# Two-layer hybrid decoder: SBUF slots claimed in a fixed order, and the opening's loads and splits rearranged

## The chip, the cores and the metric

One core of a Trainium2 chip (trn2). The metric is device time in microseconds (us) of one execution, as the median of several runs. Of one execution there is also a profile, with the start and length of every instruction and DMA packet.

## What is computed

A decoder of two layers over 256 tokens of width 1024, all in float32. Cut to what matters:

```python
for l in range(2):
    h = rmsnorm(x, norm_mix[l])                      # x is (1, 256, 1024)
    proj = h @ w_in[l]                               # 1024 x 5956, split into 12 parts
    # indexer parts -> rope -> scores -> 64 best keys per query
    # attention over these keys, q and k normed and roped  -> y_attn
    # HGRN2 gated linear recurrence, 4 heads of 128        -> y_hgrn
    merged = sigmoid(ga) * (y_attn @ w_proj_attn[l]) + sigmoid(gb) * (y_hgrn @ w_proj_hgrn[l])
    x = x + merged @ w_out[l]                        # 1024 x 1024
    g, u = split(rmsnorm(x, norm_ffn[l]) @ w_ffn_in[l])   # 1024 x 5632
    x = x + (silu(g) * u) @ w_ffn_out[l]             # 2816 x 1024
```

The rope angles come from `positions` (256 integers) times 32 inverse frequencies, by sine and cosine.

## The kernel before, in words

Tokens are taken as two row tiles (`i` = 0, 1) of 128. Each weight matrix is read once, in chunks (`take`): a chunk lands in a `w` tile, ScalarE rounds it to `hi` (type fp32r), VectorE subtracts to get `lo`, and each 128 x 128 by 128 x 512 product is three TensorE matmuls (`mm3`): hi weights by hi activations, lo weights by hi activations, hi weights by lo activations. The weight chunk is the moving operand; the transposed activations, split in the same way, are the stationary one. They lie in slots of the tag `hT` (normed input, attention output, merged, second norm) or `s4` (`act`, the FFN's inner activations). There are 3,024 such matmuls of 512 columns, and 96 of 324 columns (`idx`, the first group of each layer; in layer 0 it comes in four chunks).

The program is recorded first and then ordered by a planner (`schedule`, `run`): it keeps one queue per engine, gives each operation a `tail` (the longest path of priced work to the end) plus its `rank`, and at each step starts, on the engine that can start first, the ready operation with the largest sum. The order it finds is fixed in the program, and each engine works through its own list in order: an instruction that waits holds all behind it on that engine. Loads go to SyncE (SP) or, if written so, to GpSimd (POOL).

SBUF memory: each operation's tiles have a tag and a slot, and `emit` asks the pool for the slot when its first user comes up in the order. Addresses therefore go up from byte 16,512 in the order of first use, each slot rounded up to 32 bytes. In the compiled kernel before, this puts the `hT` slots at bytes 67,520, 79,808, 105,408, 117,696 (multiples of 64) and 179,168, 183,264, 203,744, 207,840 (multiples of 64 plus 32); of the `act` tiles some slots are of the first kind, some of the second. Of the 3,024 matmuls of 512 columns, 1,008 have a stationary operand of the second kind. In layer 0's FFN these are all with `i` = 1 (`h2T` of row tile 1 at 203,744 and 207,840), half of its `fi` matmuls; in layer 1's FFN none of the `fi` matmuls. The weight slots `hi` and `lo` all start at odd multiples of 64. The 324-column chunks hold rows of 1,296 bytes, so their moving operands start at steps of 16 bytes within 64.

The opening, up to the first `idx` matmul (lines 525 to 711): `ident` (for transposes), `grow` (norm weights) and the input `x` in three loads are issued on SP, then the weight chunks `w0`, `w1`, ...; nine small loads (positions `posi`, frequencies `invf`, masks `mi`, `vis`, `odd`, norm weights `qkn`, `rows`) on POOL. `WARM` = 24 matmuls of zeros (`gate`) are given the lowest rank and fill TensorE's gaps. Each quarter of `x` (row tile `i`, half `g`) is transposed on TensorE and split from PSUM in four pieces of 128 columns: `hT_hi` on ScalarE and `hT_lo` on VectorE, both with the norm weight of the piece (`gcol`) as scale. VectorE casts `posi` to `posf` and works out the angle tables (`ang`, `kk`, `cosang`, `rc`, `rs`, masks `cm`).

Of the kernel before, what the change touches and what calls it, by code (L numbers as in the profile page):

```python
# [26 lines left out]
N_IDX = 324  # L27
C_HQ, C_HF, C_HV, C_HG, C_GA, C_GB = 1860, 2372, 2884, 3396, 3908, 4932
FIRST = {(0, C_IDX): 2, (0, C_AQ): 2}
WARM = 24  # L30
LEVELS = (2, 4, 8)
TWO_PI = 2.0 * np.pi

# [120 lines left out]
class Program:  # L154
# [98 lines left out]


    def latency(self, a, b):
        if a.eng in ("SP", "POOL") and a.calls[0][0] == "dma_start":
            return self.LAT_DMA
        if a.eng == b.eng:
            return 0.0 if a.eng == "PE" else self.LAT_OWN
        return self.LAT  # L260
# [36 lines left out]
    def run(self, bonus):  # L297
# [63 lines left out]
        while len(order) < len(ops):  # L361
            best = None
            for e, lst in avail.items():
                cand = []
                for o in lst:
                    if o.blocked == releases and o.order != first_left:
                        continue
                    st = slot_time(o)
                    if st is not None:
                        cand.append((max(free[e], ready_at[o], st), o))  # L370
                while cand:
                    t0 = min(c[0] for c in cand)
                    if best is not None and t0 >= best[0]:
                        break
                    here = [(o.tail + o.extra + (bonus if e == "ACT" and o.table in (None, table) else 0.0), -o.order, o)
                            for at, o in cand if at <= t0 + 1.0]
                    o = max(here)[2]
                    if o.order != first_left and any(t.slot is None for t in o.tiles) and not safe(o):
                        o.blocked = releases
                        cand = [c for c in cand if c[1] is not o]  # L380
                        continue
                    best = (t0, o)
                    break
            if best is None:
                raise RuntimeError("no instruction can start")
            t0, o = best
            e = o.eng
            avail[e].remove(o)
            cost = o.cost
            if e == "ACT" and o.table not in (None, table):  # L390
                table = o.table
                cost += self.TABLE
            if o.calls[0][0] == "dma_start":
                begin = max(t0 + 1100.0, dma_free)
                end = begin + cost
                dma_free = end
                free[e] = t0 + (475.0 if e == "SP" else 1040.0)
            else:
                end = t0 + cost
                free[e] = end  # L400
            o.start, o.end, o.done = t0, end, True
            while first_left < len(ops) and ops[first_left].done:
                first_left += 1
            order.append(o)
            for t in o.tiles:
                if t.slot is None:
                    fr = slots[t.tag]
                    fr.sort()
                    t.slot = max((x for x in fr if x[0] <= t0 + 1.0), default=fr[0])[1]
                    fr[:] = [x for x in fr if x[1] != t.slot]  # L410
                    o.first.append(t)
                    live.add(t)
                t.left -= 1
                t.end = max(t.end, end + (self.LAT_DMA if o.calls[0][0] == "dma_start" else self.LAT))
                if t.left == 0:
                    slots[t.tag].append((t.end, t.slot))
                    live.discard(t)
                    releases += 1
            for s in o.succs:
                todo[s] -= 1  # L420
                ready_at[s] = max(ready_at[s], end + self.latency(o, s))
                if not todo[s]:
                    avail[s.eng].append(s)
# [2 lines left out]
        return self.span  # L426


    def emit(self, tc):
        nc = tc.nc  # L430
        engines = {"DVE": nc.vector, "ACT": nc.scalar, "PE": nc.tensor, "SP": nc.sync, "POOL": nc.gpsimd}
        with ExitStack() as ctx:
            sb = ctx.enter_context(tc.tile_pool(name="sb", bufs=1))
            ps = ctx.enter_context(tc.tile_pool(name="ps", bufs=1, space=PSUM))
            ctx.enter_context(tc.manual_schedule())
            real = lambda v: v.resolve() if isinstance(v, View) else v
            for o in self.order:
                for t in o.first:
                    pool = ps if t.tag in PSUM_TAGS else sb
                    t.handle = pool.tile([128] + list(t.shape), t.dtype, tag=f"{t.tag}_{t.slot}", name=t.name)  # L440
                for name, a, k in o.calls:
                    getattr(engines[o.eng], name)(*[real(x) for x in a], **{n: real(x) for n, x in k.items()})  # L442


PSUM_TAGS = ("P", "Q")
SLOTS = {"w": 3, "hi": 3, "lo": 3, "hT": 8, "s4": 14, "s2": 6, "sm": 14, "work": 2, "bias": 2, "rqs": 4,
         "gbc": 2, "P": 4, "Q": 4}
TUNING = {"stretch": 1.5, "bonus": 3000.0, "slack": 4000.0}
# [2 lines left out]
def hybrid_trunk(prog, x_d, pos_d, w_in, w_pa, w_ph, w_out, n_mix, n_ffn,  # L451
# [73 lines left out]

    x = const("x", [NT, D], F32)
    ident = const("ident", [128], F32)
    vis = const("vis", [256], F32)
    cm = const("cm", [4, 512], U8)
    odd = const("odd", [64])  # L530
    gbc = {}

    def load_g(key, src):
# [7 lines left out]

    zero = tmp("zero", [256], BF16)
    V.memset(zero, 0.0)
    touch = small("touch")
    S.activation(touch[:, 0:1], zero[:, 0:1], AF.Copy)
    gate = bank("gate")
    for _ in range(WARM):
        PE.matmul(gate[:, 0:256], zero[:, 0:128], zero, start=True, stop=True)
    prog.rank = 2e6
    grow = tmp("grow", [128])  # L550
    SP.dma_start(grow[0:8, :], n_mix[0].rearrange("(k d) -> k d", k=8))
    SP.dma_start(ident, cf_d[:, 0:128])
    prog.rank = 1e6
    for g in range(2):
        gs = slice(g * 512, (g + 1) * 512)
        SP.dma_start(x[:, 0, gs], x_d[0, 0:128, gs])
    SP.dma_start(x[:, 1, :], x_d[0, 128:256, :])
    prog.rank = 0.0
    neg = const("neg", [256], F32)


# [31 lines left out]
    def norm_half(i, g, gkey, hT, ssq, tag):  # L593

        xs = x[:, i, g * 512:(g + 1) * 512]
        pt = bank(f"xT{i}{g}", tag)
        pv = pt.rearrange("p (k t) -> p k t", k=4)
        if gkey is None:
            transpose4(pt, xs)
            for k in range(4):  # L600
                split_to(hT[i][0][:, g * 4 + k, :], hT[i][1][:, g * 4 + k, :], pv[:, k, :], gcol[:, g * 4 + k:g * 4 + k + 1])
        else:
            xg = tmp(f"xg{i}{g}", [512])
            V.tensor_tensor(xg, xs, gbc[gkey][:, g * 512:(g + 1) * 512], op=ALU.mult)
            transpose4(pt, xg)
            split_to(hT[i][0][:, g * 4:g * 4 + 4, :], hT[i][1][:, g * 4:g * 4 + 4, :], pv)
        junk = tmp(f"sq{i}{g}", [512])
        S.activation(junk, xs, AF.Square, accum_out=ssq[:, g:g + 1])

# [8 lines left out]
    gcol = const("gcol", [8])  # L618
    V.tensor_copy(gcol, growp[:, 0:8])
    hT = pair("hT0")  # L620
    R = []
    for i in range(NT):
        ssq = small(f"ss{i}")
        for g in range(2):
            norm_half(i, g, None, hT, ssq, "P")
        R.append(norm_scale(ssq, f"r{i}"))


    mi = tmp("mi", [320], I32)
    posi = const("posi", [NT], I32)  # L630
    POOL.dma_start(posi, pos_d.rearrange("o (i p) -> p (o i)", p=128))
    invf = const("invf", [32], F32)
    POOL.dma_start(invf, invf_d[0].partition_broadcast(128))
    qkn = const("qkn", [2, DEPTH, 64], F32)
    POOL.dma_start(qkn[:, 0], q_norm.partition_broadcast(128))
    POOL.dma_start(qkn[:, 1], k_norm.partition_broadcast(128))
    POOL.dma_start(vis, cf_d[:, 128:384])
    POOL.dma_start(mi, cm_d)
    POOL.dma_start(odd, cf_d[:, 384:448])
    rows = tmp("rows", [128])  # L640
    V.memset(rows, 0.0)
    POOL.dma_start(rows[0:8, :], h_lb.rearrange("l (h d) -> (l h) d", h=4))
    POOL.dma_start(rows[8:10, :], h_norm)

    V.tensor_scalar(neg, vis, -1.0, BIG, op0=ALU.add, op1=ALU.mult)
    for a in range(3):
        V.tensor_copy(cm[:, a, :].rearrange("p (h t) -> p h t", h=8), mi[:, None, a * 64:a * 64 + 64].to_broadcast([128, 8, 64]))
    V.tensor_copy(cm[:, 3, :].rearrange("p (h t) -> p h t", h=4), mi[:, None, 192:320].to_broadcast([128, 4, 128]))
    posf = small("posf")
    V.tensor_copy(posf[:, 0:NT], posi)  # L650
    ang = tmp("ang", [NT, 32])
    for i in range(NT):
        V.tensor_scalar(ang[:, i, :], invf, posf[:, i:i + 1], None, op0=ALU.mult)
# [25 lines left out]
    for l in range(DEPTH):  # L679
        for a in range(2):  # L680
# [4 lines left out]
                V.tensor_tensor(s_t[:, i, 0:32], IS[:, i, 0:32], qkn[:, a, l, 32:64], op=ALU.mult)  # L685
                V.tensor_tensor(s_t[:, i, 32:64], IS[:, i, 32:64], qkn[:, a, l, 0:32], op=ALU.mult)
            rtab[l, a] = (c_t, s_t)

    colp = bank("colp")
    PE.transpose(colp[:, 0:128], rows, ident)  # L690
    cols = const("cols", [16], F32)
    V.tensor_copy(cols[:, 0:10], colp[:, 0:10])
    lbt = const("lbt", [16], F32)
    V.tensor_tensor(lbt[:, 8:12], cols[:, 0:4], cols[:, 4:8], op=ALU.max)
    V.tensor_tensor(lbt[:, 0:4], cols[:, 0:4], lbt[:, 8:12], op=ALU.subtract)
# [480 lines left out]
```

## Time and profile before

| | |
|---|---|
| Median of 3 runs | 821.86 us (820.89 to 822.17) |
| The profiled execution's own time | 822.42 us |
| Its span in the trace | 820.5 us |
| Mean granted TensorE clock | 0.992 |
| HBM traffic | 137.95 MB read, 169 GB/s over the span |

"Busy" is the time in which an engine worked on at least one instruction; matmuls overlap in the records, so the length of one (0.39 us) is more than the distance from its start to the next one's start. What a matmul costs in a stream is that distance. The granted clock is the share of 2.4 GHz that TensorE had: 1.00 or 0.50 (1.2 GHz).

### The profile page before, as it was taken

To read this page: it belongs to the slowest core of one execution; us is meant where nothing else is said; L and a number is where in the kernel's file an instruction comes from. 1 tells how busy PE (TensorE), PEld (TensorE's weight loads), DVE (VectorE), ACT (ScalarE), POOL (GpSimd) and SP (SyncE) were. 2 spreads that over 40 slices of the span, in tenths; PEclk is the share of its full clock that TensorE was granted. 3 is DMA by queue.
4 is the path that set the end of the run, shared out by engine and by line. 5 is a ranking of instruction groups with operands and counts; after the bars stand their busy time and mean duration, and the time that the engine had idled before them with its cause. 6 is when DMAs were issued, how large, how long until landed. Compare 5 with 4: busy or idle time off the path is not lost.

```text
span 820.5 us, 10255 instructions
## 1 busy us (share of the span) xinstructions
PE 807.7 (98%) x3982; PEld 659.8 (80%) x3982; DVE 537.8 (66%) x947; ACT 403.2 (49%) x518; POOL 5.3 (1%) x13
## 2 busy tenths in 40 slices
PE   7999999999999999999999999999999999999998
PEld 5887788888878888888887778888887888888886
DVE  5999855677775454554488998566868645556442
ACT  5765855343364445452346676533435544445330
POOL 2000000000000000000000000000000000000000
PEclk7999999999999999999999999999999999999999
DMA  8645455333656556546546365543354665655531
GB/s 277 207 148 203 146 174 196 103 112 123 218 190 204 175 185 194 167 153 206 166 154 231 103 206 189 170 146 112 103 195 155 214 198 166 201 179 180 175 133 51
DMA packets 86224, 139.66 MB, mean 170 GB/s; under 512 B 3214, under 2 KB 50480, under 8 KB 86176
## 3 DMA queue, kind: packets, MB, share of 16 engines
q1 hardware_dynamic: 85856, 138.53, 50.9%
q0 software_dynamic: 320, 0.48, 0.3%
q8 instruction: 31, 0.51, 0.3%
q14 instruction: 17, 0.14, 0.0%
HBM read 137.95 MB, written 1.05 MB: 169 GB/s over the span
## 4 chain that ended last, share of the span: by engine, by line
PE 89%; DVE 6%; issue 2%; ACT 2%; DMA 1%; POOL 0%; DVEq 0%; POOLq 0%
PE fi L442 29%; PE fo L442 15%; PE pj L442 5%; PE gb L442 5%; PE wo L442 5%; PE ga L442 4%; PE av L442 3%; PE aq L442 3%; PE hg L442 3%; PE vh L442 3%; PE hq L442 2%; DVE lo L442 2%; PE ak L442 2%; PE idx L442 2%; PE hf L442 1%
## 5 line engine op out<-in xcount | busy, mean ns | idle before, releaser
L442 DVE TENSOR_TENSOR lo<-w,hi 128x2048 fp32r<-128x2048 f32 (+3 forms) x134 | 295.0, 2202 | 222.0 <-ACT hi L442 221.6
L442 ACT ACTIVATE hi<-w 128x2048 fp32r<-128x2048 f32 (+3 forms) x134 | 247.4, 1846 | 284.7 <-PE fi L442 96.4
L442 PE MATMUL fi<-hi,h2T_hi 128*128 128x512 f32 x352 | 141.1, 401 | 0.2
L442 PE MATMUL fi<-hi,h2T_lo 128*128 128x512 f32 x352 | 138.2, 393 | 0.0
L442 PE MATMUL fi<-lo,h2T_hi 128*128 128x512 f32 x352 | 137.7, 391 | 0.0
L442 PE MATMUL fo<-hi,act 128*128 128x512 f32 x352 | 111.4, 395 | 0.0
L442 PEld LDWEIGHTS fi<-hi,h2T_lo 128*128 128x128 f32 x352 | 66.1, 188 | 15.3 <-DVE h2T_lo L442 0.7
L442 PEld LDWEIGHTS fo<-hi,act 128*128 128x128 f32 x352 | 66.1, 188 | 14.9
L442 PEld LDWEIGHTS fi<-hi,h2T_hi 128*128 128x128 f32 x352 | 66.1, 188 | 13.8 <-DVE h2T_lo L442 0.8
L442 PEld LDWEIGHTS fi<-lo,h2T_hi 128*128 128x128 f32 x352 | 66.2, 188 | 13.2
L442 PE MATMUL fo<-lo,act 128*128 128x512 f32 x176 | 69.1, 392 | 0.0
L442 PEld LDWEIGHTS fo<-lo,act 128*128 128x128 f32 x176 | 33.1, 188 | 7.4
L442 PE MATMUL gb<-hi,hT_hi 128*128 128x512 f32 x64 | 26.8, 418 | 0.0
L442 PE MATMUL pj<-hi,yT_hi 128*128 128x512 f32 x64 | 26.0, 407 | 0.0
L442 PE MATMUL wo<-hi,mT_hi 128*128 128x512 f32 x64 | 25.8, 404 | 0.0
L442 PE MATMUL ga<-hi,hT_hi 128*128 128x512 f32 x64 | 25.7, 402 | 0.0
L442 PE MATMUL pj<-hi,yT_lo 128*128 128x512 f32 x64 | 25.3, 395 | 0.0
L442 PE MATMUL pj<-lo,yT_hi 128*128 128x512 f32 x64 | 25.2, 394 | 0.0
L442 PE MATMUL gb<-hi,hT_lo 128*128 128x512 f32 x64 | 25.2, 393 | 0.0
L442 PE MATMUL ga<-hi,hT_lo 128*128 128x512 f32 x64 | 25.1, 393 | 0.0
L442 PE MATMUL wo<-lo,mT_hi 128*128 128x512 f32 x64 | 25.1, 392 | 0.0
L442 PE MATMUL ga<-lo,hT_hi 128*128 128x512 f32 x64 | 25.1, 392 | 0.0
(346 smaller groups left out, 1309.9 us busy)
## 6 DMA issues: line engine op xcount, KB each, us to landing
w<-in_w_ffn_in_dram SPq DMA_DIRECT2D x88, 512.0 KB, 4.7
w<-in_w_in_dram SPq DMA_DIRECT2D x42, 1024.0 KB, 5.1
w<-in_w_ffn_out_dram SPq DMA_DIRECT2D x22, 1024.0 KB, 4.7
w<-in_w_out_dram SPq DMA_DIRECT2D x8, 1024.0 KB, 4.7
w<-in_w_proj_attn_dram SPq DMA_DIRECT2D x4, 1024.0 KB, 4.9
w<-in_w_proj_hgrn_dram SPq DMA_DIRECT2D x4, 1024.0 KB, 4.9
w<-in_w_in_dram SPq DMA_DIRECT2D x4, 512.0 KB, 11.4
w<-in_w_in_dram SPq DMA_DIRECT2D x4, 324.0 KB, 10.8
```

Of the source, the lines that this page charges most:

```text
L442: getattr(engines[o.eng], name)(*[real(x) for x in a], **{n: real(x) for n, x in k.items()})
```

## The change

1. A new method `homes` is called before the first instruction: it claims all SBUF slots in a chosen order. Slots are sorted by size; the small ones fill bytes 16,512 to 24,576, then come `w`, `hi`, `lo` (8,192 bytes each), `hT`, `s4`, `gbc` (4,096 bytes each) from 24,576 on, so that each of these starts at a multiple of 4,096; then the rest.
2. `ident` and `grow` are loaded from ScalarE's queue. `x` is loaded in four quarters; the first goes ahead of everything on SP, the other three get ranks just under those of `w0`, `w1`, `w2`.
3. The small loads move from POOL to SP, with a rank between those of `w1` and `w2`. `vis`, `odd` and `invf` become parts of one tile, `table`.
4. The first splits: transposes of one quarter, one VectorE multiply of 128 x 512 by `gcol` into SBUF (`xg`), one ScalarE copy to `hT_hi`, one subtract to `hT_lo` - on VectorE for the first quarter, on GpSimd for the other three. The squares for the norm come after all of them.
5. Positions are loaded as two rows of 128 integers into the tile that also holds `rows`, converted on GpSimd, turned into columns by the transpose that `rows` needs anyway, and copied out on VectorE.
6. `WARM` is 28; the planner counts ScalarE's DMA issues as it does SP's.

```diff
-WARM = 24
+WARM = 28
...
+    def homes(self, pool):
+        size = {}
+        for tag, q in self.queue.items():
+            for t in q:
+                if tag not in PSUM_TAGS:
+                    key = (tag, t.slot)
+                    size[key] = max(size.get(key, 0), t.n * SIZE.get(t.dtype, 4))
+        big = [k for tag in ("w", "hi", "lo", "hT", "s4", "gbc") for k in sorted(size) if k[0] == tag]
+        rest = sorted((k for k in size if k not in big), key=lambda k: (size[k], k))
+        at, low = BASE, []
+        for k in rest:
+            n = -(-size[k] // 32) * 32
+            if at + n <= ORIGIN:
+                low.append((k, size[k]))
+                at += n
+        low.reverse()
+        named = {k for k, _ in low}
+        if at < ORIGIN:
+            low.append((("pad", 0), ORIGIN - at))
+        for (tag, slot), n in low + [(k, size[k]) for k in big + [k for k in reversed(rest) if k not in named]]:
+            pool.tile([128, -(-n // 4)], F32, tag=f"{tag}_{slot}", name=f"home_{tag}{slot}")
...
+            self.homes(sb)
...
+BASE, ORIGIN = 16512, 24576
...
+    prog.rank = 2e6
+    S.dma_start(ident, cf_d[:, 0:128])
+    S.dma_start(grow[0:8, :], n_mix[0].rearrange("(k d) -> k d", k=8))
+    for g in range(2):
+        for i in range(NT):
+            prog.rank = (2e6, 499500.0)[g + i > 0] - 1e3 * (2 * g + i - 1)
+            gs = slice(g * 512, (g + 1) * 512)
+            SP.dma_start(x[:, i, gs], x_d[0, i * 128:(i + 1) * 128, gs])
...
-            for k in range(4):
-                split_to(hT[i][0][:, g * 4 + k, :], hT[i][1][:, g * 4 + k, :], pv[:, k, :], gcol[:, g * 4 + k:g * 4 + k + 1])
...
+    for g in range(2):
+        ks = slice(g * 4, g * 4 + 4)
+        for i in range(NT):
+            pt = bank(f"xT{i}{g}", "P")
+            transpose4(pt, x[:, i, g * 512:(g + 1) * 512])
+            xg = tmp(f"xg{i}{g}", [4, 128])
+            V.tensor_tensor(xg, pt.rearrange("p (k t) -> p k t", k=4), gcol[:, ks, None].to_broadcast([128, 4, 128]), op=ALU.mult)
+            first_hi = S.activation(hT[i][0][:, ks, :], xg, AF.Copy)
+            E = V if g == 0 and i == 0 else POOL
+            E.tensor_tensor(hT[i][1][:, ks, :], xg, hT[i][0][:, ks, :].bitcast(F32), op=ALU.subtract)
...
+        prog.after = first_hi
+            S.activation(junk, x[:, i, g * 512:(g + 1) * 512], AF.Square, accum_out=ssq[:, g:g + 1])
...
-    POOL.dma_start(posi, pos_d.rearrange("o (i p) -> p (o i)", p=128))
-    POOL.dma_start(invf, invf_d[0].partition_broadcast(128))
...
+    prog.rank = 5e5 - 1e3 * 1.5
+    SP.dma_start(rows[0:8, :], h_lb.rearrange("l (h d) -> (l h) d", h=4))
+    SP.dma_start(rows[8:10, :], h_norm)
+    SP.dma_start(posi[32:34, :], pos_d.rearrange("o (i p) -> (o i) p", p=128))
+    SP.dma_start(table[:, 320:352], invf_d[0].partition_broadcast(128))
+    SP.dma_start(table[:, 0:320], cf_d[:, 128:448])
+    SP.dma_start(mi, cm_d)
+    SP.dma_start(qkn[:, 0], q_norm.partition_broadcast(128))
+    SP.dma_start(qkn[:, 1], k_norm.partition_broadcast(128))
...
+    POOL.tensor_copy(rows[32:34, :], posi[32:34, :])
+    PE.transpose(colp[:, 0:128], rows, ident)
+    V.tensor_copy(cols[:, 0:10], colp[:, 0:10])
+    V.tensor_copy(posf[:, 0:NT], colp[:, 32:32 + NT])
```

## Rows read from the trace of the kernel before

**Rows 1.** Page, busy time, share of the span and instructions of each engine.
```profile
PE 807.7 (98%) x3982; PEld 659.8 (80%) x3982; DVE 537.8 (66%) x947; ACT 403.2 (49%) x518; POOL 5.3 (1%) x13
```
**Rows 2.** Page, the chain of work that ended last, by engine.
```profile
PE 89%; DVE 6%; issue 2%; ACT 2%; DMA 1%; POOL 0%; DVEq 0%; POOLq 0%
```
**Rows 3.** Windows: stretch, length, then each engine's busy time, clock, DMA.
```profile
0.00:5.80 5.80, 4.74 (x22) 3.13 (x22) 0.54 (x4) 2.21 (x4) 4.75 (x12) 1.00 0.38 104
5.80:9.20 3.40, 1.44 (x11) 0.88 (x9) 0.84 (x5) 1.50 (x5) 0.56 (x2) 1.00 0.88 271
9.20:19.50 10.30, 7.75 (x28) 6.89 (x29) 8.67 (x28) 7.66 (x21) 0.00 (x0) 0.51 1.05 365
...
60.00:63.80 3.80, 1.66 (x13) 1.24 (x11) 3.80 (x11) 2.94 (x3) 0.00 (x0) 1.00 0.00 0
63.80:67.30 3.50, 3.50 (x12) 2.73 (x10) 3.50 (x20) 2.89 (x5) 0.00 (x0) 0.52 0.67 209
67.30:82.00 14.70, 14.70 (x80) 11.96 (x79) 14.70 (x45) 6.81 (x7) 0.00 (x0) 1.00 0.67 233
```
**Rows 4.** Timeline, opening: start, length, engine, instruction, idle before and what ended it.
```profile
1.59 1.30 SPq L442 DMA_DIRECT2D x<-in_x_dram  x3
...
2.94 13.03 SPq L442 DMA_DIRECT2D w<-in_w_in_dram  x11
...
4.76 1.06 PE L442 MATMUL xT<-ident,x 128*128 128x128 f32 x4
4.91 0.17 DVE L442 CAST posf<-posi 128x2 f32<-128x2 int32 x1 [3.77 <-DMA posi<-in_positions_dram]
...
8.25 0.39 DVE L442 TENSOR_SCALAR ang<-invf,posf 128x32 f32<-128x32 f32 x2 [3.11 <-DMA invf<-in_invf_dram]
...
9.80 1.97 PE L442 MATMUL xT<-ident,x 128*128 128x128 f32 x8 [2.54 <-DMA x<-in_x_dram]
...
12.51 0.74 ACT L442 ACTIVATE hi<-w 128x648 fp32r<-128x648 f32 x1
...
13.41 0.61 PE L442 MATMUL idx<-hi,hT_hi 128*128 128x324 f32 x1 [1.21 <-DVE hT_lo L442]
```
**Rows 5.** Chain in order of time: start, length, link (first two `idx`/`aq` links).
```profile
14.75 9.41 PE idx L442 x47
24.16 5.48 PE aq L442 x24
```
**Rows 6.** DMA, 0 to 40 us: GB/s in 40 slices of 1 us; then time to landing.
```profile
GB/s 0 39 51 288 164 68 85 360 392 381 344 260 322 388 392 389 387 389 385 389 383 387 389 389 395 350 268 133 27 0 0 0 96 262 412 279 0 0 41 209
...
x<-in_x_dram SPq DMA_DIRECT2D x2, 256.0 KB, 3.5
```
**Rows 7.** Lines of VectorE, 0 to 82 us: count, busy and mean ns, idle before.
```profile
L442 DVE SCALAR_TENSOR_TENSOR hT_lo<-xT,gcol,hT_hi 128x128 fp32r<-128x128 f32 x16 | 4.6, 343 | 0.9 <-ACT hT_hi L442 0.9
...
L442 DVE TENSOR_TENSOR rot<-raw,rc 128x512 f32<-128x512 f32 x4 | 2.7, 678 | 0.0
```
**Rows 8.** Timeline of TensorE, `idx`: the first and last of 12, then of 23.
```profile
16.27 0.47 PE L442 MATMUL idx<-hi,hT_hi 128*128 128x324 f32 x1
...
19.24 0.47 PE L442 MATMUL idx<-hi,hT_lo 128*128 128x324 f32 x1
...
20.58 0.31 PE L442 MATMUL idx<-lo,hT_hi 128*128 128x324 f32 x1
...
23.85 0.31 PE L442 MATMUL idx<-hi,hT_lo 128*128 128x324 f32 x1
```
**Rows 9.** Timeline of TensorE, layer 0's FFN: each first of 12 matmuls.
```profile
303.01 0.39 PE L442 MATMUL fi<-hi,h2T_hi 128*128 128x512 f32 x1
...
305.74 0.39 PE L442 MATMUL fi<-hi,h2T_hi 128*128 128x512 f32 x1
...
308.53 0.39 PE L442 MATMUL fi<-hi,h2T_hi 128*128 128x512 f32 x1
```
**Rows 10.** Chain in order of time, the same stage in layer 0 and layer 1.
```profile
301.77 8.29 PE fi L442 x36
...
678.70 8.19 PE fi L442 x36
```

More of the change, by code (lines that the diff above doesn't have):

```diff
@@ L255, in latency @@
     def latency(self, a, b):
-        if a.eng in ("SP", "POOL") and a.calls[0][0] == "dma_start":
+        if a.eng in ("SP", "POOL", "ACT") and a.calls[0][0] == "dma_start":
             return self.LAT_DMA
@@ L396, in run @@
                 dma_free = end
-                free[e] = t0 + (475.0 if e == "SP" else 1040.0)
+                free[e] = t0 + (1040.0 if e == "POOL" else 475.0)
             else:
@@ L445 @@
 PSUM_TAGS = ("P", "Q")
+SIZE = {U8: 1, BF16: 2}
+BASE, ORIGIN = 16512, 24576
 SLOTS = {"w": 3, "hi": 3, "lo": 3, "hT": 8, "s4": 14, "s2": 6, "sm": 14, "work": 2, "bias": 2, "rqs": 4,
@@ L527, in hybrid_trunk @@
     ident = const("ident", [128], F32)
-    vis = const("vis", [256], F32)
+    table = const("table", [352], F32)
+    vis, odd, invf = table[:, 0:256], table[:, 256:320], table[:, 320:352]
     cm = const("cm", [4, 512], U8)
-    odd = const("odd", [64])
     gbc = {}
@@ L543, in hybrid_trunk @@
     V.memset(zero, 0.0)
+    prog.rank = 2e6
+    grow = tmp("grow", [128])
+    S.dma_start(ident, cf_d[:, 0:128])
[5 more added lines that the diff above has]
+            SP.dma_start(x[:, i, gs], x_d[0, i * 128:(i + 1) * 128, gs])
+    prog.rank = 0.0
     touch = small("touch")
@@ L548, in hybrid_trunk @@
         PE.matmul(gate[:, 0:256], zero[:, 0:128], zero, start=True, stop=True)
[L549 to L558, printed above, removed]
     neg = const("neg", [256], F32)
@@ L597, in norm_half @@
         pv = pt.rearrange("p (k t) -> p k t", k=4)
-        if gkey is None:
-            transpose4(pt, xs)
-            for k in range(4):
-                split_to(hT[i][0][:, g * 4 + k, :], hT[i][1][:, g * 4 + k, :], pv[:, k, :], gcol[:, g * 4 + k:g * 4 + k + 1])
[L602 to L606, printed above, removed]
+        xg = tmp(f"xg{i}{g}", [512])
+        V.tensor_tensor(xg, xs, gbc[gkey][:, g * 512:(g + 1) * 512], op=ALU.mult)
+        transpose4(pt, xg)
+        split_to(hT[i][0][:, g * 4:g * 4 + 4, :], hT[i][1][:, g * 4:g * 4 + 4, :], pv)
         junk = tmp(f"sq{i}{g}", [512])
@@ L623, in hybrid_trunk @@
         ssq = small(f"ss{i}")
+        prog.after = first_hi
         for g in range(2):
-            norm_half(i, g, None, hT, ssq, "P")
+            junk = tmp(f"sq{i}{g}", [512])
+            S.activation(junk, x[:, i, g * 512:(g + 1) * 512], AF.Square, accum_out=ssq[:, g:g + 1])
+        prog.after = None
         R.append(norm_scale(ssq, f"r{i}"))
     mi = tmp("mi", [320], I32)
-    posi = const("posi", [NT], I32)
-    POOL.dma_start(posi, pos_d.rearrange("o (i p) -> p (o i)", p=128))
-    invf = const("invf", [32], F32)
-    POOL.dma_start(invf, invf_d[0].partition_broadcast(128))
     qkn = const("qkn", [2, DEPTH, 64], F32)
[L635 to L639, printed above, removed]
     rows = tmp("rows", [128])
+    posi = tmp("posi", [128], I32)
     V.memset(rows, 0.0)
-    POOL.dma_start(rows[0:8, :], h_lb.rearrange("l (h d) -> (l h) d", h=4))
-    POOL.dma_start(rows[8:10, :], h_norm)
+    prog.rank = 5e5 - 1e3 * 1.5
[7 more added lines that the diff above has]
+    SP.dma_start(qkn[:, 1], k_norm.partition_broadcast(128))
+    prog.rank = 0.0
+    POOL.tensor_copy(rows[32:34, :], posi[32:34, :])
+    colp = bank("colp")
+    PE.transpose(colp[:, 0:128], rows, ident)
+    cols = const("cols", [16], F32)
+    V.tensor_copy(cols[:, 0:10], colp[:, 0:10])
+    posf = small("posf")
+    V.tensor_copy(posf[:, 0:NT], colp[:, 32:32 + NT])
     V.tensor_scalar(neg, vis, -1.0, BIG, op0=ALU.add, op1=ALU.mult)
@@ L648, in hybrid_trunk @@
     V.tensor_copy(cm[:, 3, :].rearrange("p (h t) -> p h t", h=4), mi[:, None, 192:320].to_broadcast([128, 4, 128]))
-    posf = small("posf")
-    V.tensor_copy(posf[:, 0:NT], posi)
     ang = tmp("ang", [NT, 32])
@@ L687, in hybrid_trunk @@
             rtab[l, a] = (c_t, s_t)
[L689 to L692, printed above, removed]
     lbt = const("lbt", [16], F32)
```

## The prediction, made before the changed kernel was run

> **What bounds the kernel now.** I read the busy shares first: TensorE (PE) works in 98% of the span, VectorE (DVE) in 66% [rows 1]. The chain of waits agrees: 89% of the time that led to the end is PE's, 6% is DVE's [rows 2]. So the time is the distance from one matmul to the next, summed, and an edit counts if it shortens that distance or takes away a stretch in which PE stands or runs at half clock. The windows show two such stretches [rows 3]. Up to 19.5 us PE is busy for 13.9 us only, and from 9.2 to 19.5 us the granted clock is 0.51, the lower of its two levels (1.2 of 2.4 GHz). From 60.0 to 63.8 us PE is busy for 1.66 us, and then runs at 0.52 for 3.5 us. From 67 to 82 us DVE has no idle time at all.
>
> The opening's timeline says why [rows 4]. DVE stands 3.77 us for the positions and 3.11 us for the frequencies, both loaded through POOL's queue, and its first split of the input waits behind them. PE's transposes of the second row tile wait for `x` until 9.80; the first product of `idx` starts at 13.41, and the steady stream at 14.75 [rows 5]. The transfers could have been faster: 164, 68 and 85 GB/s in the slices from 4 to 7 us, against 380 to 392 later, while POOL's small loads are under way [rows 6].
>
> **Part 1, the addresses.** In layer 0's FFN the same `hi` and `lo` weights run first against row tile 0, then against row tile 1. The twelve matmuls of tile 0 take 305.74 - 303.01 = 2.73 us, 227.5 ns each; those of tile 1 take 308.53 - 305.74 = 2.79 us, 232.5 ns each [rows 9]. Moving operand, shape and clock are the same; what differs is the stationary address, a multiple of 64 for tile 0 and 32 past one for tile 1. The other check is across layers: 36 `fi` matmuls, half of them with the odd address, take 8.29 us in layer 0; 36 with none take 8.19 us in layer 1 [rows 10]. That is 0.10 / 18 = 5.6 ns each. I take 5.0 ns. After the change every `hT` and `s4` slot starts at a multiple of 4,096, so all 1,008 matmuls lose it: 1,008 x 5.0 ns = 5.0 us, and with PE's 89% of the chain [rows 2] **4.5 us**. Bounds: 0 (if the odd slots are slow for another reason, say that they lie high in memory) and 1,008 x 5.6 = 5.6 us. For the moving operand I take nothing: in `idx` it starts at steps of 16 bytes within 64, and 23 products from 20.58 to 23.85 us keep one pace (3.27 / 22 = 149 ns, the 12 before at half clock 2.97 / 11 = 270 ns) [rows 8]. No row shows a moving operand at a multiple of 128, so this stays a rival below.
>
> **Part 2, the opening, step by step.** *Loads of x.* The three issues of `x` take 1.30 us, 0.43 each [rows 4]. With two loads gone to ScalarE's queue, the first quarter is issued 0.87 us earlier, at 0.7; it lands 3.5 us after issue [rows 6], at 4.2. `w0` is issued second, at 1.2 instead of 2.94 [rows 4], with 0.33 MB of its own behind 0.26 MB. At 389 GB/s [rows 6] that is 1.5 us after the first bytes, so it is there by 5.5. ScalarE issues two DMAs ahead of its own work, about 0.9 us in a stretch in which it is busy 2.2 of 5.8 us [rows 3]: nothing, unless it is late for the first copy at 6 us.
>
> *First splits.* Transposes 1.06 us [rows 4], to 5.3. `xg` on DVE is a 128 x 512 with two operands, 0.68 us in the nearest row [rows 7]; the copy to `hT_hi` I set at the same 0.68, and the subtract too: 6.0, 6.7, 7.3. `hi` of `w0` takes 0.74 us [rows 4] and lies beside this. So `idx` starts at about 7.0 instead of 13.41, and the product that needs `hT_lo` at 7.4. The sixteen pieces of 343 ns on DVE (5.5 us) become five operations of 0.68 (3.4 us) [rows 7].
>
> *GpSimd's three subtracts.* The trace has no arithmetic on POOL. Bounds: DVE's 0.68 us [rows 7] and four times that, 2.7; I take 1.2, nearer the lower end. The second quarter (row tile 1) lands at about 5.3, is split by 8.4, and its `hT_lo` comes at 9.6, while PE could use it at 8.1: 1.5 us of waiting. The other two are needed two chunks later and lie beside products.
>
> The Trainium skill speaks against this step. "GPSIMD Engine Reference", section "Elementwise - side-by-side cycle accounting", gives 4,497 ns for such an operation of 2,048 elements on GpSimd, 1.96 times VectorE's; an estimate from it for 512 elements is 1.1 to 1.3 us. "SBUF - State Buffer", section "SBUF: two separate sides", says that a VectorE operation with two SBUF inputs and a GpSimd operation that reads SBUF shut each other out for a whole instruction; by that the sum would be the 814.0 of the first rival below. No row here shows the two side by side.
>
> *Clock.* PE stood from its last `gate` to 9.80 waiting for `x` [rows 4], and the clock fell [rows 3]. After, 28 gates of about 0.2 us, the transposes and then `idx` leave no such gap before 8 us. If the clock is up as it was from 5.8 us [rows 3], the 48 products take 48 x 149 ns = 7.2 us; at half clock 48 x 270 ns = 13.0 [rows 8]. I take the first: 7.0 + 7.2 + 1.5 = 15.7, and 0.3 for a chunk that comes late: `idx` ends at 16.0 instead of 24.16 [rows 5], **8.2 us** earlier.
>
> *Small loads.* Eight issues on SP are 8 x 0.43 = 3.4 us of its queue and 0.47 MB, 1.2 us at 389 GB/s. Their rank puts them right after `w1`, but the plan adds the path length, and that of the tables is shorter than that of the first chunks; so they come somewhere behind `w2` to `w5`. SP runs ahead of the transfers there (eleven issues in 13.03 us [rows 4]), so the cost is between 0 and 3.4 us on the chunks behind, which PE needs only from 16 us on; I take 0. The positions now go SP, GpSimd, transpose, two copies, and DVE's angle work waits in order behind them, with splits of weights behind that. In the kernel before, the two such waits took 6.9 us [rows 4]; bounds 0 and 6.9, I take 0.3, already counted.
>
> *How much of it stays.* DVE is full in the rows after the opening [rows 3], so PE can't run further ahead than DVE does. DVE idled 19.5 - 10.05 = 9.45 us up to 19.5 us [rows 3]; now it starts at 5.3, so it can be 4.1 us ahead by idle time and 5.5 - 3.4 = 2.1 us by less work: 6.2 us. Were all DVE work urgent, 6.2 would stay; the top-k search isn't, so it lies between 6.2 and 8.2. I take **7.0 us**. Bounds 3 (both GpSimd and position waits near their upper ends) and 9.
>
> **Sum.** 822.42 (the profiled execution) - 4.5 - 7.0 = 810.9; the median of the runs is 0.56 lower, so **810.4 us**. The stall at 60 us could vanish with the new order (2.1 us of standing and 3.5 / 2 = 1.7 us of clock [rows 3]) or come back elsewhere; I take 0 for it and put 4 us in the range.
>
> **Rivals.** *GpSimd's subtracts hold DVE up.* If DVE's splits of the first chunks, which read two SBUF tiles as the subtracts do, wait while these run, DVE loses 3 x 1.2 = 3.6 us when all behind it is late: 814.0. For it: DVE is in order and nearly full from 9.2 us on, 8.67 of 10.30 us [rows 3]. Against: no row shows one engine slowed by the other. 12%.
>
> *The clock falls again in the opening* (GpSimd's late subtracts or a late quarter leave PE a hole): +5.8 us by the two paces, 816.2. For it: it fell in the kernel before after one hole [rows 3]. Against: the wait that I see is 1.5 us, not the 2.54 of before [rows 4]. 17%.
>
> *The addresses do nothing*: 814.9. For it: all slow slots but some `act` slots lie high. Against: `fi` shows the step with equal weights [rows 9], and it recurs across layers [rows 10]. 8%.
>
> *Full alignment is worth more*: at 2.4 GHz 512 columns are 213 ns, the best rows show 227.5 [rows 9, 10]. If the 64-byte remainder of the weight slots makes up all of this, 3,024 x 14 ns x 0.89 = 38 us more: 772. For it: nothing in the trace says what the 14 ns are. Against: `idx` keeps its pace at any 16-byte step [rows 8]. 5%. "TensorE: Matmul & The Clock Gate" of the Trainium skill, section "Wait - 56ns, not 53.3ns?", gives columns / 2.4 GHz + 2.5 ns, 215.7 ns for 512; by that it would be 32 us, 778. The trace disagrees for this type of matmul: 227.5 ns at a full clock.
>
> *Slower: PE catches up with DVE.* Place: 20 to 75 us, where DVE has no idle time. Pulled 8 us closer, PE runs dry whenever a split or an evacuation comes late; each time it costs what the place at 60 us cost, 2.1 + 1.7 = 3.8 us [rows 3]. From the fourth on it outweighs 11.5 us; with four it is 822.42 - 11.5 + 15.2, 825.6 in the median. For it: DVE's full windows. Against: the plan weighs splits above the search, and the chain shows no such place in `idx` and the first `aq` [rows 5]. 5%.
>
> **How the numbers follow.** Forecast 50%, its own range 804 to 813 (opening 5 to 9, addresses 4 to 5.6, the place at 60 us); GpSimd 12%, the clock 17%, no address effect 8%, more alignment 5%, slower 5%, no change 3%. The range 803 to 818 holds the first four but for their tails, 82%. A change under 0.2% (1.6 us) can't be told from none here. Faster 92%, within 3%, slower 5%.
>
> **What would show it.** The twelve `fi` matmuls of row tile 1 in layer 0 at 227 to 228 ns, as those of tile 0; 36 `fi` at 8.2 us in both layers. The first `idx` at 6.5 to 8 us, the first `aq` at 14 to 18, granted clock 1.00 from 6 to 20 us, GB/s near 380 from 4 us on. It is wrong if `fi` keeps two paces, if `idx` shows 270 ns for long, or if PE has new holes of over 2 us between 20 and 80 us.

## The result, and the profile after

The changed kernel takes 814.47 us in the median of four runs (814.07 to 815.19); the kernel before, run beside it on the same chip, 821.38 (820.71 to 822.17). The ratio is 0.9917 (95% interval 0.9899 to 0.9934): 6.9 us less, where 11.5 were forecast. The span falls from 820.5 to 813.4 us, so the profiled pair shows 7.1 us of it.

The busy shares of the changed kernel answer to [rows 1]:

```profile
PE 801.3 (99%) x3986; PEld 657.3 (81%) x3986; DVE 537.6 (66%) x936; ACT 400.9 (49%) x506; POOL 6.5 (1%) x8
```

and the chain of waits, by engine, to [rows 2]:

```profile
PE 84%; DVE 10%; issue 2%; ACT 2%; DMA 0%; POOL 0%; POOLq 0%; ACTq 0%; DVEq 0%
```

DVE's share of the chain has grown from 6 to 10%: PE now stands closer behind DVE, and waits for it more often (10 times instead of 7, 4.6 us instead of 4.0 over the whole trace). The windows say where (stretch, length, busy time of PE, PEld, DVE, ACT and POOL, granted clock, DMA share, GB/s):

```profile
0.00:5.10 5.10, 3.88 (x17) 2.50 (x17) 0.31 (x2) 1.49 (x2) 0.20 (x4) 1.00 0.55 175
5.10:19.50 14.40, 12.65 (x83) 11.30 (x83) 11.77 (x20) 10.60 (x19) 6.32 (x4) 1.00 1.02 364
...
55.00:59.70 4.70, 1.90 (x12) 1.22 (x10) 4.70 (x18) 4.06 (x4) 0.00 (x0) 1.00 0.01 2
59.70:66.50 6.80, 6.18 (x15) 4.83 (x16) 6.80 (x34) 1.78 (x4) 0.00 (x0) 0.50 0.47 154
66.50:82.00 15.50, 15.50 (x87) 12.31 (x85) 13.97 (x34) 9.07 (x15) 0.00 (x0) 1.00 0.56 181
```

Against [rows 3], the opening's half clock (0.51 from 9.2 to 19.5 us) is gone: full clock from 5.1 us on. But the other hole is still there, at 55 us instead of 60, and in this execution what follows it is longer: 6.8 us at half clock instead of 3.5. That length isn't a property of the new order. Experiment e5 below, which has the same order of instructions on PE and the same time (814.41 us), shows 3.5 us at half clock at the same place in its trace:

```profile
60.30:63.80 3.50, 3.35 (x8) 2.68 (x9) 3.50 (x22) 1.30 (x3) 0.00 (x0) 0.51 0.62 181
```

The changed kernel's trace, with 3.3 us more at half clock, is 1.2 us longer here than e5's: its first `hq` starts at 58.57 against 58.69, its first `av` at 76.33 against 75.25.

The opening's timeline (start, length, engine, instruction, idle before it and what ended it) answers to [rows 4] and [rows 5]:

```profile
0.73 0.86 SPq L467 DMA_DIRECT2D x<-in_x_dram  x2
1.65 0.94 SPq L467 DMA_DIRECT2D w<-in_w_in_dram  x2
...
4.17 1.08 PE L467 MATMUL xT<-ident,x 128*128 128x128 f32 x4 [0.17 <-DMA ident<-in_cf_dram]
...
6.02 0.74 ACT L467 ACTIVATE hi<-w 128x648 fp32r<-128x648 f32 x1 [2.73 <-DMA w<-in_w_in_dram]
...
7.78 0.63 PE L467 MATMUL xT<-ident,x 128*128 128x128 f32 x4 [0.63 <-DVE lo L467]
...
8.27 0.39 PE L467 MATMUL idx<-hi,hT_hi 128*128 128x324 f32 x1
...
13.24 0.41 PE L467 MATMUL idx<-hi,hT_lo 128*128 128x324 f32 x1 [0.44 <-POOL hT_lo L467]
```

How far the changed kernel is ahead at the same matmul, from the starts in both traces, tells where the 7.1 us come from:

| matmul | before | after | ahead |
|---|---|---|---|
| first `idx`, layer 0 | 13.41 | 8.27 | 5.1 |
| first `aq` | 24.00 | 17.65 | 6.35 |
| first `hf` | 48.78 | 43.05 | 5.7 |
| first `hq` | 63.79 | 58.57 | 5.2 |
| first `av` | 78.18 | 76.33 | 1.85 |
| first `vh`, layer 0 | 93.06 | 90.75 | 2.3 |
| first `fi`, layer 0 | 228.58 | 225.75 | 2.8 |
| first `fo`, layer 0 | 356.11 | 351.90 | 4.2 |
| first `fi`, layer 1 | 629.23 | 623.03 | 6.2 |
| last `fo`, layer 1 | 816.35 | 809.18 | 7.2 |

So the opening gains 6.35 us. Some 1.1 of them are gone by the first `hq`, the stretch from 58 to 76 us takes 3.4 more, and 2.3 are left at the first `vh`. From there the lead grows by 4.9 us, most of it where the kernel before had stationary tiles at odd addresses (32 past a multiple of 64; even means a multiple of 64), as in layer 0's `fi`.

### The profile page after: what moved, and what is told of

Read it like the earlier page. It is cut to its first block, busy times and chain, and to the rows that moved or that the text cites. A ratio compares the mean times of both kernels' runs of the same rounds, so it can differ in the third digit from the quotient of the medians.

```text
span 813.4 us, 10251 instructions
## 1 busy us (share of the span) xinstructions
PE 801.3 (99%) x3986; PEld 657.3 (81%) x3986; DVE 537.6 (66%) x936; ACT 400.9 (49%) x506; POOL 6.5 (1%) x8
## 4 chain that ended last, share of the span: by engine, by line
PE 84%; DVE 10%; issue 2%; ACT 2%; DMA 0%; POOL 0%; POOLq 0%; ACTq 0%; DVEq 0%
PE fi L467 29%; PE fo L467 15%; PE pj L467 5%; PE gb L467 5%; PE wo L467 5%; PE ga L467 4%; DVE lo L467 4%; PE av L467 3%; PE hg L467 3%; PE vh L467 3%; PE hq L467 2%; DVE work L467 2%; PE aq L467 1%; ACT hi L467 1%; PE fp L467 1%
## 5 line engine op out<-in xcount | busy, mean ns | idle before, releaser
L467 PE MATMUL gb<-lo,hT_hi 128*128 128x512 f32 x64 | 25.0, 391 | 0.0
```

## The experiments

Twelve kernels, each run beside the kernel before. On the addresses, theory A is Part 1 of the prediction (a stationary tile off a multiple of 64 is slow by itself); its rivals are the moving operand, more alignment, and the two operands' addresses against each other. On the opening, theory B is that the lead is eaten at 55 us because one weight split stands late in DVE's order; its rival is that DVE has too much work there in any order.

| run | median us | before beside it | ratio (95%) |
|---|---|---|---|
| e1_homes_only | 816.87 | 822.05 | 0.9936 (0.9921 to 0.9951) |
| e2_opening_only | 824.36 | 822.05 | 1.0027 (1.0017 to 1.0036) |
| e3_stationary_32 | 827.92 | 822.05 | 1.0070 (1.0055 to 1.0085) |
| e4_moving_32 | 827.74 | 822.05 | 1.0069 (1.0054 to 1.0084) |
| e5_all_64 | 814.41 | 822.09 | 0.9911 (0.9894 to 0.9927) |
| e6_lo_first | 807.36 | 822.09 | 0.9824 (0.9809 to 0.9838) |
| e7_lo_first_before | 816.34 | 822.09 | 0.9931 (0.9916 to 0.9946) |
| e8_subtract_dve | 819.38 | 822.09 | 0.9971 (0.9960 to 0.9982) |
| e9_small_on_pool | 814.81 | 821.97 | 0.9913 (0.9898 to 0.9927) |
| e10_all_32 | 814.63 | 821.97 | 0.9914 (0.9899 to 0.9929) |
| e11_dve_lo_first | 804.50 | 821.97 | 0.9787 (0.9771 to 0.9804) |
| e12_homes_lo_first | 811.32 | 821.97 | 0.9873 (0.9859 to 0.9888) |

### Each part alone

**e1**, the kernel before with the claimed slots:

```diff
+    def homes(self, pool):
...
+            self.homes(sb)
```

> The kernel before with only the claims in a fixed order (every slot of weights and activations at a multiple of 4,096). Address theory (1,008 matmuls lose 5 ns each because their stationary address becomes a multiple of 64): 4.9 us faster than before, 816.5. Rival (the 4.9 us after 82 us came from the new order of work, not from addresses): 821.4. The opening should be as before: first idx product at 13.4 us.

**e2**, the changed kernel without them:

```diff
-            self.homes(sb)
```

> The changed kernel without the fixed claims: slots again lie in the order of first use, which the new opening shifts, so that now 1,896 of the 3,024 matmuls have a stationary address 32 past a multiple of 64, and all a moving address of that kind. Stationary theory: 1,896 x 5 ns = 9.5 us slower than the changed kernel, 824, so slower than the kernel before in spite of the faster opening. If moving addresses cost as much again: 829 to 834. Rival (addresses don't matter): 814.5 to 815.

e1 gives 5.2 us, all of it without touching the opening (its first `aq` starts at 24.03, as before). e2 has its first `aq` at 18.18 and is nevertheless 2.3 us slower than before. The two parts don't add up: without fixed slots, the new order of the opening also claims the slots in another order. In e2, 1,896 of the 3,024 matmuls have a stationary tile 32 past a multiple of 64 (1,008 before), and every moving one is there too, at 96 past a multiple of 128.

### Which operand's address

**e3** puts `hT` and `s4` (stationary) 32 bytes past a multiple of 64, **e4** `hi` and `lo` (moving) in their stead:

```diff
-        big = [... ("w", "hi", "lo", "hT", "s4", "gbc") ...]
+        big = [... ("w", "hi", "lo", "gbc", "hT", "s4") ...]   # e3: 32 bytes claimed ahead of hT, 32 after s4
+        big = [... ("w", "hT", "s4", "gbc", "hi", "lo") ...]   # e4: 32 bytes claimed ahead of hi, 32 after lo
```

> The changed kernel with all slots of the stationary operands (hT, s4) 32 bytes past a multiple of 4,096, the weight slots at multiples of 4,096; same order of work. Stationary theory: 3,024 x 5 ns = 15 us slower than the changed kernel, 829; every fi matmul at 232 to 233 ns. Rival (moving operand, or how high a slot lies): 814.5.

> The changed kernel with the weight slots (hi, lo: the moving operands) 32 bytes past a multiple of 4,096 and the stationary ones at multiples of 4,096, low in memory; same order of work. Stationary theory: no change, 814.5, fi at 227 to 228 ns. Rival (any operand counts): up to 15 us slower, 829.

**e5** moves all six groups by 64 bytes (multiples of 64, no longer of 128), **e10** all by 32 (both operands odd):

```diff
-            low.append((("pad", 0), ORIGIN - at))
+            low.append((("pad", 0), ORIGIN - at + 64))   # e5
+            low.append((("pad", 0), ORIGIN - at + 32))   # e10
```

> The changed kernel with all large slots 64 bytes past a multiple of 4,096 (odd multiples of 64). Theory (a multiple of 64 is all that counts): 814.5, fi at 227 to 228 ns. Rival (more alignment, 128 bytes and up, is worth something too): slower than the changed kernel by 1 ns or more per matmul, 817.5 or more.

> The changed kernel with all large slots, moving and stationary, 32 bytes past a multiple of 4,096. Theory 1 (what costs 5 ns is that the two operands' addresses differ by 32 modulo 64): no change, 814.5, 228 ns per fi matmul. Theory 2 (each operand that starts 32 past a multiple of 64 costs by itself, the two together at least as much as one): 827.8 or more, 233 ns. The opening-only kernel, with a mixture, had 230.6 ns where both were odd; if that holds here: 822.

The order of instructions on PE is the same in the changed kernel and in these four. e3 and e4 cost the same, 13.4 us over the changed kernel by the medians, 13.4 / 3,024 = 4.4 ns a matmul; e5 and e10 cost nothing. So neither a stationary nor a moving tile at 32 past is slow by itself: the pair is, where the two differ by 32 modulo 64. The chain of each shows the same 36 `fi` matmuls of layer 0 (start, length, link). The changed kernel, in both layers (to be read against 8.29 and 8.19 in [rows 10]):

```profile
286.58 8.20 PE fi L467 x36
...
672.47 8.20 PE fi L467 x36
```

e3, the stationary operand moved:

```profile
290.06 8.39 PE fi L472 x36
```

e4, the moving one:

```profile
289.18 8.38 PE fi L472 x36
```

e10, both:

```profile
286.23 8.20 PE fi L467 x36
```

The mean from one start to the next of 512-column matmuls after 82 us (some 2,580 intervals in each trace) says it in ns: after, e1, e5 and e10 228, e3 and e4 233.2, before 230.0 (228.4 with the stationary tile at a multiple of 64, 232.9 without).

e2 shows that this isn't the whole rule. There the two operands differ by 32 modulo 64 in 3,024 - 1,896 = 1,128 matmuls, which at 5.2 ns explain 5.9 of the 9.9 us that e2 is behind the changed kernel. The 1,896 pairs that agree should cost nothing, and yet take 230.6 ns from start to start and not 228. Why, no run shows.

### What takes the opening's lead back

The timeline of the changed kernel around the hole:

```profile
43.25 1.92 ACT L467 ACTIVATE hi<-w 128x2048 fp32r<-128x2048 f32 x1 [0.76 <-PE ak L467]
...
55.41 0.60 PE L467 MATMUL hfp<-ident,hfraw 128*128 128x128 f32 x4
...
55.62 1.91 ACT L467 ACTIVATE hi<-w 128x2048 fp32r<-128x2048 f32 x1 [0.79 <-PE hf L467]
...
57.43 0.67 ACT L467 ACTIVATE hfraw<-hf,r1y 128x512 f32<-128x512 f32 x1
...
57.98 2.29 DVE L467 TENSOR_TENSOR lo<-w,hi 128x2048 fp32r<-128x2048 f32 x1
58.16 0.66 PE L467 MATMUL hfp<-ident,hfraw 128*128 128x128 f32 x4 [2.14 <-ACT hfraw L467]
58.57 0.47 PE L467 MATMUL hq<-hi,hT_hi 128*128 128x512 f32 x1
...
60.32 0.79 PE L467 MATMUL hq<-lo,hT_hi 128*128 128x512 f32 x1 [1.28 <-DVE lo L467]
```

PE stands 2.14 us for an ACT copy (`hfraw`) that stands behind ACT's 1.91 us weight copy, and 1.28 us more for the split that DVE starts at 57.98, although its `hi` (the line at 43.25) has been there for 12.8 us: DVE's order puts it behind rope and top-k work. In the kernel before only the first of the two showed. **e6** ranks the weight splits, this one and all others, above the other work of DVE in the changed kernel, **e7** does so in the kernel before, **e12** in e1:

```diff
+        prog.rank = 1e4
         V.tensor_tensor(lo, w, hi, ...)
+        prog.rank = 0.0
```

> The changed kernel with a rank of 10,000 on the splits lo of the weights, so that the plan puts them ahead of the top-k search and the rope work on VectorE; nothing else changed. Theory (the opening's lead of 6.4 us is paid back at 55 to 73 us because a split stands late in VectorE's order, TensorE waits 2.4 and 1.75 us and falls to half clock for 6.8 us): these holes go, 4 to 5 us faster, 809.5 to 810.5. Rival (VectorE has no time left there, whatever its order): TensorE waits elsewhere, 813.5 or more.

> The kernel before with the same rank on the splits. It has the same hole at 61 to 63 us and half clock to 67 us. Theory (order alone): 3.8 us for the hole and 0.4 for 96 fewer matmuls with a stationary address 32 past a multiple of 64: 817.2. Rival (VectorE has no time left): 821.

> The kernel before with the fixed claims and the splits ranked first, without the new opening. Theory (address, order and opening add up once no hole eats the lead): 816.34 less 912 x 5 ns = 4.5 us, 811.8, so that the opening is worth 4.5 us against 807.36. Rival (the lead is limited by VectorE's total work, at 2.4 us): 809.7.

The split in question in e6, 0.6 us after its `hi`, and PE's timeline in it:

```profile
46.67 2.28 DVE L467 TENSOR_TENSOR lo<-w,hi 128x2048 fp32r<-128x2048 f32 x1
```

```profile
55.09 0.39 PE L467 MATMUL hf<-hi,hT_lo 128*128 128x512 f32 x1
55.31 0.39 PE L467 MATMUL hq<-hi,hT_hi 128*128 128x512 f32 x1
...
90.43 0.60 PE L467 MATMUL hfp<-ident,hfraw 128*128 128x128 f32 x4
```

Windows of e6:

```profile
55.00:59.70 4.70, 4.70 (x25) 3.86 (x24) 4.70 (x12) 3.45 (x4) 0.00 (x0) 1.00 0.15 20
59.70:66.50 6.80, 6.80 (x32) 5.63 (x31) 6.80 (x25) 2.49 (x2) 0.00 (x0) 1.00 0.37 141
66.50:82.00 15.50, 15.35 (x85) 11.85 (x84) 15.50 (x56) 10.41 (x22) 0.00 (x0) 1.00 0.46 141
```

The hole and the half clock are gone, while DVE is as full as before: it was the order of the work and not the amount of DVE's. That the place of this one split alone did it is not shown. The rank made the planner reorder the other engines too: the `hfp` transposes, on which PE stood for the first 2.14 us, come at 90 us in e6, and `hq` follows `hf` without them. By the times in the changed kernel's timeline both were needed: with the transposes moved alone, `hq` would still have waited for the split until 60.26, and with the split early alone, PE would still have stood for `hfraw`. No run moves one of them alone.

e6 takes 7.1 us off the changed kernel (814.47 to 807.36), more than the 4 to 5 expected. The trace prices the place at 2.14 + 1.28 of standing and 6.8 / 2 of half clock, 6.8 us, and by e5's 3.5 us of half clock at 5.2. e7 takes 5.75 off the kernel before (some 0.4 of it may be addresses, as 912 stationary tiles are odd in it and not 1,008; its first `aq` is 0.7 earlier, at 23.29). With the rank on both sides, the new opening is worth 811.32 - 807.36 = 4.0 us, of 22.75 - 17.98 = 4.8 us at the first `aq`; without it, 816.87 - 814.47 = 2.4, of 6.4.

### The subtracts on GpSimd

POOL's timeline in the changed kernel:

```profile
7.88 1.53 POOL L467 TENSOR_TENSOR hT_lo<-xg,hT_hi 128x512 fp32r<-128x512 f32 x1 [7.44 <-ACT hT_hi L467]
11.45 3.57 POOL L467 TENSOR_TENSOR hT_lo<-xg,hT_hi 128x512 fp32r<-128x512 f32 x2 [2.03 <-ACT hT_hi L467]
```

and DVE's over the same stretch:

```profile
6.85 0.82 DVE L467 TENSOR_TENSOR lo<-w,hi 128x648 fp32r<-128x648 f32 x1
7.59 0.68 DVE L467 TENSOR_TENSOR hT_lo<-xg,hT_hi 128x512 fp32r<-128x512 f32 x1
8.47 1.63 DVE L467 TENSOR_TENSOR lo<-w,hi 128x648 fp32r<-128x648 f32 x1 [0.20 <-ACT hi L467]
...
11.22 0.82 DVE L467 TENSOR_TENSOR lo<-w,hi 128x648 fp32r<-128x648 f32 x1
12.63 1.25 DVE L467 TENSOR_TENSOR lo<-w,hi 128x648 fp32r<-128x648 f32 x1 [0.59 <-ACT hi L467]
```

The same split takes DVE 0.82 us when it starts with POOL at rest, and 1.63 and 1.25 us when it starts while a subtract runs. The subtracts took 1.53, 1.74 and 1.87 us. If each waits for the other's instruction to end, the three leave 9.41 - 8.27 = 1.14, 13.19 - 12.04 = 1.15 and 15.02 - 13.88 = 1.14 us of their own, and the two late splits 0.69 each after the subtract has ended: one price each. (Where a split was running first, as at 11.22, it kept its 0.82.) **e8** takes the subtracts off GpSimd, **e11** does so with the splits ranked first:

```diff
-            E = V if g == 0 and i == 0 else POOL
+            E = V
```

> The changed kernel with all four first subtracts on VectorE, none on GpSimd. In the changed kernel TensorE waits 0.71 and 0.94 us for GpSimd's, which take 1.5 to 1.9 us. Theory A (the lead is paid back later anyway): the first aq product 1 to 1.6 us earlier than 17.65, the total within 1 us of 814.5. Theory B (each microsecond of lead stays): 813. Theory C (VectorE loses more by 3 x 0.68 us than TensorE wins): 815.5 or more.

> The changed kernel with the weight splits ranked first on VectorE and all four first subtracts on VectorE. Theory (order on VectorE decided both results: 807.36 with the rank, 819.38 with the subtracts alone): the 1.3 us that the subtracts gave at aq stay, 806. Rival (VectorE has no time for three more operations): 808 or more.

The lines of DVE from 5 to 17 us (count, busy and mean ns, idle before) have the four splits in the changed kernel at

```profile
L467 DVE TENSOR_TENSOR lo<-w,hi 128x648 fp32r<-128x648 f32 x4 | 4.5, 1130 | 0.8 <-ACT hi L467 0.8
```

and in e11 all at the short price, the subtracts now among them:

```profile
L467 DVE TENSOR_TENSOR lo<-w,hi 128x648 fp32r<-128x648 f32 x4 | 3.3, 822 | 0.0
L467 DVE TENSOR_TENSOR hT_lo<-xg,hT_hi 128x512 fp32r<-128x512 f32 x4 | 2.7, 705 | 0.0
```

e8's opening is the best of all, its first `aq` at 16.32 instead of 17.65, and it ends 4.9 us behind the changed kernel. Its windows say where:

```profile
59.70:66.50 6.80, 6.80 (x37) 5.55 (x35) 6.80 (x22) 4.09 (x5) 0.00 (x0) 1.00 0.00 0
66.50:82.00 15.50, 8.43 (x31) 6.05 (x30) 15.50 (x56) 8.43 (x13) 0.00 (x0) 0.67 0.21 68
```

and PE's timeline in it, for what:

```profile
68.84 0.66 PE L467 MATMUL hfp<-ident,hfraw 128*128 128x128 f32 x4 [2.12 <-ACT hfraw L467]
...
71.98 1.12 PE L467 MATMUL hqp<-ident,hqraw 128*128 128x128 f32 x4 [1.91 <-ACT hqraw L467]
...
75.47 1.08 PE L467 MATMUL qkp<-ident,rot 128*128 128x128 f32 x4 [2.37 <-DVE n11y L467]
```

The plan came out with another order: PE runs through to 66 us, where its main products are over 10 us ahead of the changed kernel's, and gives it all back in three holes and at a clock of 0.67. With the splits first (e11) none of them is left, and the same edit is worth 807.36 - 804.50 = 2.9 us. Only 0.4 of these are there at the first `aq` (17.54 against 17.98 in e6); the rest comes behind it, with another new order:

```profile
66.50:82.00 15.50, 15.50 (x72) 12.90 (x71) 11.93 (x37) 8.22 (x9) 0.00 (x0) 1.00 0.66 209
```

e11, 804.50 us, is the fastest version, 17.5 us ahead of the kernel before.

### The small loads

**e9** puts the eight small loads back on GpSimd's queue:

```diff
-    SP.dma_start(rows[0:8, :], ...)
+    POOL.dma_start(rows[0:8, :], ...)      # and the seven behind it
```

> The changed kernel with its eight small loads issued by GpSimd (POOL) again, ahead of GpSimd's subtracts; x, the weights and the splits as changed. Theory (half of the opening's gain came from clearing POOL's small loads off the transfers and out of VectorE's way): the first aq product at 19 to 21 us instead of 17.65, GB/s lower in the slices before 8 us. Rival (the order of x and the weights on SP, and fewer pieces, were all): aq at 17 to 18 us. The total follows the new order of work behind it and is read only beside the lead: 813 to 818.

The first `aq` on PE's timeline in the changed kernel:

```profile
17.65 0.40 PE L467 MATMUL aq<-hi,hT_hi 128*128 128x512 f32 x1
```

and in e9:

```profile
20.16 0.40 PE L467 MATMUL aq<-hi,hT_hi 128*128 128x512 f32 x1
```

The queue is worth 2.5 us of the opening. Behind the hole, at the first `av`, e9 is level with the changed kernel's trace again (76.29 against 76.33), and its total is the same within the intervals. Part of that is the clock of the two executions: e9's ran 3.5 us at half clock there, as e5's did, and its first `av` is 1.0 us behind e5's 75.25. So of the 2.5 us lost ahead of the hole about 1 at most is left behind it, which agrees with theory B.

## Why the prediction came out as it did

The time, 814.5, lies inside the range and 4 us above the forecast, 1.5 us outside the likeliest case's own range (804 to 813). Faster was right. That the range holds the time is partly luck: the gain of the opening fell below its own bounds, and the 4 us put in for the place at 60 us made up for it. By its steps:

- **Part 1, the addresses: size right, rule half.** Forecast 4.5; measured 4.9 in the traces (from the first `vh` to the end) and 5.2 in e1. Layer 0's `fi` fell to 8.20 us as in layer 1, as "What would show it" said. But "for the moving operand I take nothing" was wrong: the weights at multiples of 64 were half of the condition (e4), and an odd stationary address is free when the moving one is odd as well (e10). That the size came out is partly luck: the claimed order aligns both operands, and the prediction gave a reason for one. "Full alignment is worth more" fell: matmuls keep 228 ns with both at multiples of 128 (after) and at odd multiples of 64 (e5). "The addresses do nothing" fell with e1.
- **Part 2, up to the first `aq`: 6.35 instead of 8.2.** The first quarter's transposes are at 4.17 to 5.25, as forecast. The first `idx` came at 8.27 and not 7.0: `w0` was there at 6.02 instead of 5.5, and the transposes of the third quarter stand ahead of it in PE's order and started at 7.78. Inside `idx`, PE waited 0.44 us (13.24, above) and 0.68 us (at 15.07) for the second and third GpSimd `hT_lo`, not for the first, as the prediction had it. "The clock falls again in the opening" did not happen: the clock is 1.00 from 5.1 to 19.5 us.
- **The rival "GpSimd's subtracts hold DVE up" was there, at a third of its price.** DVE lost (1.63 - 0.82) + (1.25 - 0.82) = 1.24 us, not 3.6. The subtract's own 1.14 us agrees with the 1.2 taken; what made it 1.53 to 1.87 is the waiting. The rule that such operations of the two engines shut each other out for a whole instruction (the Trainium skill, "SBUF - State Buffer", section "SBUF: two separate sides") is what these rows show. It cost less here because only two splits started while a subtract ran. That this rival's 814.0 us is nearer to the measured time than the forecast is an accident: what was missing was lost at 55 us and not here.
- **"How much of it stays" is the step that failed: 2.4 us instead of 7.0.** The bounds there, 3 to 9, don't hold the value. The sum counted DVE's idle time and work up to 19.5 us and asked whether DVE as a whole could run ahead. The limit was the order of the work around one place: a split that DVE starts 12.8 us after its `hi`, and transposes that stand in PE's order ahead of `hq`. e6 removes the hole with DVE as full as before. "The place at 60 us, I take 0 for it" was in truth a term of the sum: PE reached it 5 us earlier and then also waited 1.28 us for `lo`, so that by the same pricing it cost 5.2 to 6.8 us (by the half clock of e5's and of the changed kernel's execution) and not 3.8. About 1.1 us of the lead went ahead of it, between the first `aq` and the first `hq`.
- **The rival "PE catches up with DVE"** named this mechanism, but with four new holes and a slower kernel; it needed one place, the old one, grown longer, which took 3.4 us of the lead. "Wrong if PE has new holes of over 2 us between 20 and 80": the hole is the old one. e8 is that rival nearly as described: three holes of about 2 us and most of the gain gone.
- **The forecast's 11.5** is nearer to what the parts are worth once the order at that place is another: e6 against e7 is 9.0 us.

Left open: why e2, where 1,896 pairs have both operands at 96 modulo 128, keeps 230.6 ns there and not 228; which of the two orders, DVE's or PE's, makes how much of e6's 7.1 us; and how much of the opening's 6.35 us the finer loads of `x` and how much the fewer, wider splits give, which no run took apart.

## What to carry to other kernels

Follow a gained lead forward to the next place where the engine stood before the change, and look at what is queued ahead of the late instruction there: in these kernels a lead was kept only as far as the order of the work let it through, and another order (one rank here) was worth more than either part of the change. Before pricing such a place from one trace, look at a second execution: the half clock behind the hole took 3.5 us in one and 6.8 in another. Give the two operands of a matmul stream fixed places with the same remainder by a large power of two (0, 32 and 64 past a multiple of 4,096 were alike here), and check the addresses after every reordering, since the order of claims moves them. Look at arithmetic that is moved to GpSimd together with what VectorE does at that moment.

## What was not expected of the hardware

- A 512-column matmul of this type took 228 ns from start to start with both operands 0, 32 or 64 past a multiple of 4,096, and 233.2 ns where the two differed by 32, whichever of them was odd. In e2, with both at 96 modulo 128, it took 230.6.
- A VectorE subtract of 128 x 648 from two SBUF tiles took 1.63 and 1.25 us beside a GpSimd subtract, 0.82 us alone; GpSimd's own went from some 1.14 to 1.87 us.
- Eight small loads on GpSimd's DMA queue instead of SyncE's (e9) delayed the first `aq` by 2.5 us.
